# Fifteen instead of ten pairs of an FFN's up projection in seven half-size products, with weight sums made by adding transfers

## The chip, the cores and the metric

One core of a Trainium2 chip runs the whole program in one launch. The engines are TensorE (PE; its weight loads are PEld), VectorE (DVE), ScalarE (ACT), GpSimd (POOL) and SyncE (SP), which here only issues transfers. The metric is device time in microseconds, the median of several runs.

## The reference

A trunk of two layers over 512 tokens of width 1024, all in float32: a gated linear recurrence in layer 0, RWKV-7 time mixing in layer 1, each followed by the same channel mixer, then a final norm. The change touches the channel mixer alone:

```python
def _conv_ffn(x, norm, w_up, conv_w, conv_b, w_down):
    h = _rmsnorm(x, norm)
    u = jnp.einsum('btd,df->btf', h, w_up)                      # 1024 -> 2 x 3072
    gate = _causal_dwconv(u[..., :D_FF], conv_w, conv_b)        # 3 taps
    hid = jax.nn.gelu(gate, approximate=True) * u[..., D_FF:]
    return jnp.einsum('btf,fd->btd', hid, w_down)               # 3072 -> 1024

for layer in range(DEPTH):                                      # DEPTH = 2
    x = x + (_rglru_block if layer % 2 == 0 else _rwkv7_block)(x, ...)
    x = x + _conv_ffn(x, ...)
return _rmsnorm(x, final_norm)
```

## The kernel before

Every float32 matrix is split into a rounded part `hi` (ScalarE, a CAST) and the rest `lo` (VectorE, a subtraction), and a product is three matmuls, `mm3` (L54): hi with hi, hi with the operand's lo, lo with hi. Weights come from memory in pieces of 512 KB (`raw`), through one tag `b4` of 21 buffers that holds pieces, split pieces and the eight operand blocks `xs`. `plan_weights` writes down the order of all pieces; `weights_load` issues their loads on SP's queue in that order; a load starts when the buffer that it was given has been let go by its last reader. Pieces of the plan marked as a pair's own are split by that pair, all others by `weights_split` and taken by `next_weights`. The framework places each engine's instructions in one fixed order; an engine works through its own in that order and waits on semaphores.

`ffn(l, ...)` works on 12 *pairs*: pair n is 256 columns of the gate half of `w_up` and the same 256 of the other half. There are two kinds.

- `Whole`: four products of 24 matmuls of 512 tokens, G0, U0 (first 512 rows of `w_up` into the banks accG and accU), G1, U1 (the other 512 rows).
- `Halves`: the four blocks (two halves of the rows, gate and up) times two halves of the tokens, H = 256, written with seven products in place of eight (Winograd's form of Strassen's scheme). Each is 24 matmuls of 256 tokens. Products are named 1, 5, 6, 2, 7, then 4, 3, in the banks accA (1, 6, 7, 4), accF (5, 3) and accD (2). Products 1, 2 and 3 read `xs`; 5, 6, 7 and 4 read sums of operand blocks (`xt`) that `operands()` makes once for each FFN. Their weights are the pieces and sums of them: four tensor_tensor on VectorE per pair before (S1, S2, one in place, S4; L726 to L729). After a product, ScalarE copies accA (`s`), VectorE combines the banks, and `gate` convolves (four scalar_tensor_tensor, L678) and applies gelu.

`HALVES = (3, 5, 7, 9, 11)` in both FFNs. In a *period* run an even pair, an odd pair and `down(n, ...)`, the down projection of the two pairs before: two groups of 512 columns of `w_down`, each of two pieces (four products of six matmuls per piece, one bank each for four blocks). After the first piece of the first group, `between` runs the odd pair's products 4 and 3; at the end of that group `then` prepares the next pair's first weights. In the second FFN VectorE adds the down projection to `xtok` (L830). `products` sets the order of products, and `ahead` places the splits of the product after the next ahead of each.

Of the kernel before, what the change touches and what calls it, by code (L numbers as in the profile page):

```python
# [16 lines left out]
P = 128  # L17
# [14 lines left out]
HALVES = (3, 5, 7, 9, 11)  # L32
# [12 lines left out]
class Kernel:  # L45
# [54 lines left out]
    def plan_weights(self):  # L100
# [4 lines left out]
        def add(w, r0, c0, k=2, quad=False):  # L105
            plan.append((w[r0 : r0 + k * P, c0 : c0 + D // k].rearrange("(k p) c -> p k c", p=P), k, quad))
# [46 lines left out]
    def weights_load(self, upto):  # L153
        while self.n_load < min(upto, len(self.plan)):
            i = self.n_load
            src, k, _ = self.plan[i]
# [419 lines left out]
    def ffn(self, l, xs, finish, after=None):  # L576
        nc, tc = self.nc, self.tc
        last = l == 1
        with tc.tile_pool(name=f"ffn{l}", bufs=1) as pool:
# [43 lines left out]
            def operands():  # L623
# [6 lines left out]
                stt = nc.vector.scalar_tensor_tensor  # L630
                for k in range(4):
# [5 lines left out]
                    stt(f[:, 0], x2[:, H:], gain(4 + k), d[:, 1], ALU.mult, ALU.add)  # L637
                    parts(t2, k, f[:, 0])
                    stt(f[:, 1], x2[:, 0:H], gain(4 + k), f[:, 0], ALU.mult, ALU.subtract)
# [22 lines left out]
            tt = nc.vector.tensor_tensor  # L662
# [51 lines left out]
            class Halves(Pair):  # L714
# [3 lines left out]
                def weights(pair, p):  # L718
                    if p == 1:
                        i = quads[pair.n]  # L720
                        self.weights_load(i + 4)
                        pair.f = dict(zip((1, 7, 4, 2), [self.loaded.pop(i + j) for j in range(4)]))
                    f = pair.f
                    if p == 1:
                        f[5], f[6], f[3] = (self.b4(F32, (4, 256), name) for name in ("S1", "S2", "S4"))
                        tt(f[5], f[7], f[4], ALU.add)  # L726
                        tt(f[6], f[5], f[1], ALU.subtract)
                        tt(f[7], f[1], f[7], ALU.subtract)
                        tt(f[3], f[6], f[2], ALU.subtract)  # L729
# [3 lines left out]
                    pair.w[p] = hi, lo  # L733

                def product(pair, p):
# [19 lines left out]
                    if p == 7:  # L755
                        tt(s[7], s[7], bank["F"], ALU.subtract)
                        tt(gp[:, :, 2 + H :], s[7], rb(H, T), ALU.mult)
                    if p == 4:
                        tt(gp[:, :, 2 : 2 + H], bank["A"], rb(0, H), ALU.mult)
                        for e in range(2):  # L760
                            pair.gate(e)
                    if p == 3:
                        tt(s[6], s[6], bank["F"], ALU.subtract)
# [8 lines left out]
            quads = self.quads[l * 12 : l * 12 + 12]  # L772
            pairs, hids = {}, []
            kind = lambda n: Halves if n in HALVES else Whole
            seq = [(n, p) for n in range(12) for part in kind(n).order for p in part]
            made, at = [0], [0]
# [9 lines left out]
            def products(upto, more=2):  # L786

                while True:
# [4 lines left out]
                    if p == "G0" and n + 1 in HALVES:  # L793
                        self.weights_load(quads[n] + 8)
# [4 lines left out]
                    if p == 7:  # L799
                        self.weights_split(quads[n] + 6)  # L800
# [58 lines left out]

            for n in range(3, 12, 2):  # L860
# [4 lines left out]
                down(n, 2 * n - 6, 4 if n < 11 else 8, lambda: products((n, 3)), lambda: ahead(at[0] + 2))  # L865
# [889 lines left out]
```

## Time and profile before

| | |
|---|---|
| median of 3 runs | 1296.62 us (1294.75 to 1297.82) |
| the profiled execution | 1296.44 us, of which the instructions' span is 1294.7 |
| PE, DVE, ACT, POOL busy | 98%, 74%, 51%, 5% of the span |
| granted TensorE clock | 0.997 |
| read from memory | 114.44 MB, 92 GB/s with the writes |

PE, DVE, ACT and POOL are the four engines' busy times; a matmul's own duration is longer than the distance to the next one, because they are pipelined, so lengths of stretches are taken from the chain of waits, which holds what ended last at every moment. SPq and POOLq are the queues of transfers that SP and GpSimd issue; "to landing" is from issue until the data is there. In a row of a timeline stand start, length, engine, line, operation, output<-inputs.

### The profile page before, as it was taken

What the parts mean: (1) busy time and instruction counts of PE and PEld (TensorE: products, weight loads), DVE (VectorE), ACT (ScalarE), POOL (GpSimd) and SP (SyncE); (2) the same over time, 40 slices, a digit from 0 to 9 for tenths busy, and PEclk for the clock granted to TensorE, in tenths of its full rate; (3) what the DMA queues carried; (4) which work ended last, traced back from release to release, by engine and by line L of the source; (5) the groups of instructions that cost most, each with busy time, mean ns of one, the idle gap of its engine ahead of it and who ended that gap; (6) DMA issues with size and microseconds to landing.
All of it is one profiled execution on the core that took longest, in us unless ns stands there. A gap on an engine that the chain in (4) does not pass through costs nothing.

```text
span 1294.7 us, 22291 instructions
## 1 busy us (share of the span) xinstructions
PE 1266.9 (98%) x9259; PEld 1068.0 (82%) x9259; DVE 962.0 (74%) x1440; ACT 662.9 (51%) x1070; POOL 64.8 (5%) x112
## 2 busy tenths in 40 slices
PE   9999999999999999999899998899999999999997
PEld 8777888989888888877678887778889898988886
DVE  5998678767676777788999867777877666676754
ACT  6797455434344343568845468655644343443442
POOL 3000000000000000010002031210000000000000
PEclk9999999999999999999999999999999999999999
DMA  7322341515151513422212112132314151505131
GB/s 221 111 58 90 98 128 36 161 35 163 33 163 32 172 41 102 155 74 76 80 41 87 54 58 83 44 99 80 106 43 153 44 165 31 175 21 178 35 130 65
DMA packets 96710, 120.40 MB, mean 93 GB/s; under 512 B 9499, under 2 KB 70629, under 8 KB 96481
## 3 DMA queue, kind: packets, MB, share of 16 engines
q1 hardware_dynamic: 95248, 117.20, 28.6%
q8 instruction: 72, 1.18, 0.4%
q10 hardware_dynamic: 576, 1.05, 0.2%
q0 software_dynamic: 784, 0.74, 0.2%
q14 instruction: 30, 0.24, 0.1%
HBM read 114.44 MB, written 4.52 MB: 92 GB/s over the span
## 4 chain that ended last, share of the span: by engine, by line
PE 85%; DVE 9%; ACT 4%; issue 2%; POOL 0%; DMA 0%; POOLq 0%; ACTq 0%; DVEq 0%
PE acc L54 27%; PE accU L54 12%; PE accG L54 12%; PE accA L54 9%; PE accF L54 4%; PE acc L827 3%; PE acc L826 3%; PE acc L825 3%; PE accD L54 2%; DVE wl L97 1%; DVE X L1280 1%; DVE mt L947 1%; PE s L1394 1%; PE pd L1476 1%; DVE DA L1278 1%
## 5 line engine op out<-in xcount | busy, mean ns | idle before, releaser
L94 ACT CAST wh<-raw 128x1024 fp32r<-128x1024 f32 (+1 forms) x161 | 165.9, 1042 | 200.9 <-PE acc L54 55.6
L97 DVE TENSOR_TENSOR wl<-raw,wh 128x1024 fp32r<-128x1024 f32 (+1 forms) x161 | 195.5, 1220 | 95.3 <-ACT wh L94 81.7
L54 PE MATMUL accG<-xs,wh 128*128 128x512 f32 x448 | 138.8, 391 | 0.0
L54 PE MATMUL accU<-xs,wh 128*128 128x512 f32 x448 | 138.6, 391 | 0.0
L54 PE MATMUL acc<-hid,wh 128*128 128x512 f32 x384 | 119.7, 395 | 0.0
L54 PEld LDWEIGHTS accG<-xs,wh 128*128 128x128 f32 x448 | 83.7, 188 | 17.4
L54 PEld LDWEIGHTS accU<-xs,wh 128*128 128x128 f32 x448 | 83.7, 188 | 17.1
L54 PE MATMUL accG<-xs,wl 128*128 128x512 f32 x224 | 87.3, 390 | 0.0
L54 PE MATMUL accU<-xs,wl 128*128 128x512 f32 x224 | 87.3, 390 | 0.0
L54 PEld LDWEIGHTS acc<-hid,wh 128*128 128x128 f32 x384 | 71.2, 188 | 17.0 <-ACT wh L94 0.3
L54 PE MATMUL accA<-xt,hi 128*128 128x256 f32 x480 | 83.4, 277 | 0.0
L54 PE MATMUL acc<-xs,wh 128*128 128x512 f32 x256 | 81.1, 398 | 0.0
L732 DVE TENSOR_TENSOR lo<-raw,hi 128x1024 fp32r<-128x1024 f32 x40 | 48.3, 1220 | 40.2 <-PE accU L54 40.2
L678 DVE SCALAR_TENSOR_TENSOR cv<-gpad,pv,cv 128x512 f32<-128x512 f32 x96 | 69.0, 747 | 12.3 <-ACT cv L676 11.8
L827 PE MATMUL acc<-wl,hid 128*128 128x512 f32 (+1 forms) x200 | 77.2, 386 | 0.0
L826 PE MATMUL acc<-wh,hid 128*128 128x512 f32 (+1 forms) x200 | 77.0, 385 | 0.0
L825 PE MATMUL acc<-wh,hid 128*128 128x512 f32 (+1 forms) x200 | 76.7, 383 | 0.0
L54 PE MATMUL acc<-hid,wl 128*128 128x512 f32 x192 | 74.8, 395 | 0.0
L54 PEld LDWEIGHTS accA<-xt,hi 128*128 128x128 f32 x480 | 73.2, 188 | 0.9
L731 ACT CAST hi<-raw 128x1024 fp32r<-128x1024 f32 x40 | 42.1, 1051 | 57.7 <-PE accG L54 49.6
L54 PE MATMUL accA<-xt,lo 128*128 128x256 f32 x240 | 66.3, 276 | 0.0
L54 PE MATMUL acc<-mix,wh 128*128 128x512 f32 x192 | 59.6, 394 | 2.9 <-ACT wh L94 2.9
(413 smaller groups left out, 2970.7 us busy)
## 6 DMA issues: line engine op xcount, KB each, us to landing
raw<-in_ffn_w_up_dram SPq DMA_DIRECT2D x96, 512.0 KB, 3.9
raw<-in_ffn_w_down_dram SPq DMA_DIRECT2D x48, 512.0 KB, 4.0
raw<-in_rwkv_w_rkv_dram SPq DMA_DIRECT2D x24, 512.0 KB, 3.7
raw<-in_lru_w_in_dram SPq DMA_DIRECT2D x16, 512.0 KB, 4.1
raw<-in_lru_w_out_dram SPq DMA_DIRECT2D x8, 512.0 KB, 3.7
raw<-in_rwkv_w_out_dram SPq DMA_DIRECT2D x8, 512.0 KB, 3.5
xd<-x SPq DMA_DIRECT2D x8, 256.0 KB, 2.0
AR<-xd SPq DMA_DIRECT2D x1, 2048.0 KB, 9.0
```

Source lines behind the costliest of these rows:

```text
L54: mm = lambda *a, **kw: self.nc.tensor.matmul(ps, *a, skip_group_check=more, **kw)
L94: put = (self.nc.vector.tensor_copy if dve else self.nc.scalar.copy)(hi, src)
L97: self.nc.vector.tensor_tensor(lo, src, hi.bitcast(F32), ALU.subtract)
L678: nc.vector.scalar_tensor_tensor(cv, pair.gp[:, e, j : j + T], cw(j), cv, ALU.mult, ALU.add)
L731: nc.scalar.copy(hi, f[p])
L732: tt(lo, f[p], hi.bitcast(F32), ALU.subtract)
L825: nc.tensor.matmul(ps, hh[:, s], wh[:, k, m], start=kk == 0, stop=False)
L826: nc.tensor.matmul(ps, hl[:, s], wh[:, k, m], start=False, stop=False)
L827: nc.tensor.matmul(ps, hh[:, s], wl[:, k, m], start=False, stop=kk == blocks - 1)
L947: nc.vector.scalar_tensor_tensor(mt[:, 1:], h[:, cb, : T - 1], self.vec("rwkv_mix", i * 8 + cb), mt[:, 1:], ALU.mult, ALU.add)
L1278: nc.vector.tensor_tensor(w, A[:, s + 1 :, s : s + 1].to_broadcast([P, n, j]), X[:, s : s + 1, 0:j].to_broadcast([P, n, j]), ALU.mult)
L1280: nc.vector.tensor_tensor(X[:, s + 1 :, 0:j], X[:, s + 1 :, 0:j], w, ALU.add)
```

## The change

What it does, in five parts.

1. `HALVES` becomes a set for each FFN: (3, 5, 7, 9, 10, 11) for the first, (3, 4, ..., 11) for the second. Pair 10 of the first and pairs 4, 6, 8, 10 of the second change from `Whole` to `Halves`.
2. The signs of the seven products are turned, so that all sums of weights are additions: 5 is a sum of two pieces, 7 of two, 6 is 5 plus 1, 3 is 6 plus 2, and 4 is a piece. Operand sums and the combination after the products take the other sign (`minus`, a few subtractions turned to additions, two multiplications by `rb` to scalar_tensor_tensor with -1).
3. Three of the four sums leave VectorE. For 5 and 7 `weights_load` loads one piece on SP's queue and issues a second transfer on GpSimd's queue that adds the other piece in place; for 3 GpSimd adds a piece onto the weights of 6 once these are split. VectorE keeps one sum, 6 (L737).
4. So a pair by halves loads five pieces on SP's queue and three on GpSimd's, eight in place of four.
5. Where both pairs of a period go by halves, the odd pair's product 1 is placed ahead of the even pair's product 4, and loads are asked for at new points (`products`, `between`, `then`).

```diff
-HALVES = (3, 5, 7, 9, 11)
+HALVES = ((3, 5, 7, 9, 10, 11), (3, 4, 5, 6, 7, 8, 9, 10, 11))
...
                 for n in range(2 * six, 2 * six + 2):
                     self.quads.append(len(plan))
-                    i = int(n in HALVES)
-                    for half, r in ((i, 0), (1 - i, 0), (0, 512), (1, 512)):
-                        add(up, r, half * DFF + n * 256, 4, bool(i))
+                    a = lambda i, j: piece(up, j * 512, (1 - i) * DFF + n * 256, 4)
+                    if n in HALVES[l]:
+                        for first, more in (((0, 0), None), ((1, 1), (1, 0)), ((0, 1), None), ((1, 0), (0, 0)), ((1, 1), None)):
+                            plan.append((a(*first), 4, True, more and a(*more)))
...
+            if more is not None:
+                self.nc.gpsimd.dma_start(raw, more, accum_op=ALU.add)
...
                 def weights(pair, p):
+                    i = quads[pair.n]
                     if p == 1:
-                        i = quads[pair.n]
                         self.weights_load(i + 4)
-                        pair.f = dict(zip((1, 7, 4, 2), [self.loaded.pop(i + j) for j in range(4)]))
+                        pair.f = dict(zip((1, 5, 2, 7), [self.loaded.pop(i + j) for j in range(4)]))
                     f = pair.f
-                    if p == 1:
-                        f[5], f[6], f[3] = (self.b4(F32, (4, 256), name) for name in ("S1", "S2", "S4"))
-                        tt(f[5], f[7], f[4], ALU.add)
-                        tt(f[6], f[5], f[1], ALU.subtract)
-                        tt(f[7], f[1], f[7], ALU.subtract)
-                        tt(f[3], f[6], f[2], ALU.subtract)
+                    if p == 6:
+                        tt(f[1], f[5], f[1], ALU.add)
+                        f[6] = f[3] = f[1]
+                    if p == 7:
+                        self.weights_load(i + 5)
+                        f[4] = self.loaded.pop(i + 4)
                     hi, lo = self.b4(F32R, (4, 256), f"hi{p}"), self.b4(F32R, (4, 256), f"lo{p}")
                     nc.scalar.copy(hi, f[p])
                     tt(lo, f[p], hi.bitcast(F32), ALU.subtract)
                     pair.w[p] = hi, lo
+                    if p == 6:
+                        nc.gpsimd.dma_start(f[3], self.plan[i + 2][0], accum_op=ALU.add)
...
-                        tt(gp[:, :, 2 + H :], s[7], rb(H, T), ALU.mult)
+                        stt(gp[:, :, 2 + H :], s[7], -1.0, rb(H, T), ALU.mult, ALU.mult)
...
+            for n in range(4, 12, 2):
+                if n in HALVES[l] and n + 1 in HALVES[l]:
+                    seq.remove((n + 1, 1))
+                    seq.insert(seq.index((n, 4)), (n + 1, 1))
...
-                    if p == "G0" and n + 1 in HALVES:
-                        self.weights_load(quads[n] + 8)
+                    if n % 2 == 0 and n + 1 in HALVES[l] and p in ("G0", 5, 2, 7):
+                        self.weights_load(quads[n + 1] + {5: 1, 2: 2}.get(p, 4))
...
-                    if p == 7:
-                        self.weights_split(quads[n] + 6)
+                    if n % 2 and p in (2, 7):
+                        (self.weights_load if p == 2 else self.weights_split)(behind[n] + 2)
...
+            def between():
+                products((n, 3))
+                if n + 1 in HALVES[l]:
+                    self.weights_load(quads[n + 1] + 2)
+            def then():
+                if len(seq) > at[0]:
+                    self.weights_split(self.n_used + 2)
+                ahead(at[0] + 2)
...
-                down(n, 2 * n - 6, 4 if n < 11 else 8, lambda: products((n, 3)), lambda: ahead(at[0] + 2))
+                down(n, 2 * n - 6, 4 if n < 11 else 8, between, then)
```

Line numbers in the following rows of before are those of the profile; those of after are some 8 to 34 higher for the same statement (L678 is L690, L732 is L744, L97 stays, L830 is L853). Names are those of the code with a buffer number: `wl` and `wh` are split pieces of `w_down`, `lo1` the lo part of the weights of product 1, `cv` the gate's convolution, `raw` a piece.

VectorE in the second FFN, inside the down projection that follows pair 5, from the odd pair's last bank to the splits for the second column group. Before (`wl158` and `wl159` are the pieces of that group, `wl160` is the next whole pair's first piece):

```order
L757 TENSOR_TENSOR gpad1_9200<-s_10457,rb_9286 128x2x256
L97 TENSOR_TENSOR wl158_10574<-raw158_10477,wh158_10573 128x1024
L97 TENSOR_TENSOR wl159_10612<-raw159_10571,wh159_10611 128x1024
L759 TENSOR_TENSOR gpad1_9200<-accA_10313,rb_9286 128x2x256
L97 TENSOR_TENSOR wl160_10618<-raw160_10609,wh160_10617 128x1024
L678 SCALAR_TENSOR_TENSOR cv_10529<-gpad1_9200,pv_78,cv_10529 128x512
L678 SCALAR_TENSOR_TENSOR cv_10534<-gpad1_9200,pv_78,cv_10534 128x512
L678 SCALAR_TENSOR_TENSOR cv_10529<-gpad1_9200,pv_78,cv_10529 128x512
L678 SCALAR_TENSOR_TENSOR cv_10534<-gpad1_9200,pv_78,cv_10534 128x512
L763 TENSOR_TENSOR s_10397<-s_10397,accF_10344 128x512
```

And now, at the same place (`raw169` and `raw170` are the first two pieces of pair 6, the second one summed by a transfer; `wl167` is the first piece of the second column group):

```order
L772 SCALAR_TENSOR_TENSOR gpad1_9293<-s_10650,rb_9379 128x2x256
L744 TENSOR_TENSOR lo1_10705<-raw169_10694,hi1_10704 128x1024
L774 SCALAR_TENSOR_TENSOR gpad1_9293<-accA_10422,rb_9379 128x2x256
L737 TENSOR_TENSOR raw169_10694<-raw170_10696,raw169_10694 128x1024
L744 TENSOR_TENSOR lo5_10745<-raw170_10696,hi5_10744 128x1024
L690 SCALAR_TENSOR_TENSOR cv_10734<-gpad1_9293,pv_78,cv_10734 128x512
L690 SCALAR_TENSOR_TENSOR cv_10739<-gpad1_9293,pv_78,cv_10739 128x512
L690 SCALAR_TENSOR_TENSOR cv_10734<-gpad1_9293,pv_78,cv_10734 128x512
L690 SCALAR_TENSOR_TENSOR cv_10739<-gpad1_9293,pv_78,cv_10739 128x512
L778 TENSOR_TENSOR s_10586<-s_10586,accF_10531 128x512
L97 TENSOR_TENSOR wl167_10781<-raw167_10666,wh167_10780 128x1024
```

The split for the second group has moved from ahead of the gate's operations to behind them, and the next pair's sum, which reads an added piece, stands ahead of both.

VectorE further on, in the even pair 6 itself. Before, a whole pair with the four sums for pair 7 ahead of it:

```order
L726 TENSOR_TENSOR S1_10745<-raw165_10709,raw166_10711 128x1024
L727 TENSOR_TENSOR S2_10746<-S1_10745,raw164_10707 128x1024
L728 TENSOR_TENSOR raw165_10709<-raw164_10707,raw165_10709 128x1024
L729 TENSOR_TENSOR S4_10747<-S2_10746,raw167_10713 128x1024
L732 TENSOR_TENSOR lo1_10753<-raw164_10707,hi1_10752 128x1024
L97 TENSOR_TENSOR wl163_10757<-raw163_10705,wh163_10756 128x1024
L702 TENSOR_TENSOR gpad0_9199<-accG_10679,rb_9286 128x512
```

And now (`raw174` and `raw175` are pair 7's first two pieces, `raw173` is pair 6's last; `lo4` and `lo3` in these rows belong to pair 6, `lo1`, `lo5`, `lo6` to pair 7):

```order
L744 TENSOR_TENSOR lo1_10977<-raw174_10936,hi1_10976 128x1024
L737 TENSOR_TENSOR raw174_10936<-raw175_10968,raw174_10936 128x1024
L744 TENSOR_TENSOR lo4_11007<-raw173_10934,hi4_11006 128x1024
L767 TENSOR_TENSOR s_10903<-s_10903,accD_10980 128x512
L744 TENSOR_TENSOR lo3_11039<-raw169_10694,hi3_11038 128x1024
L744 TENSOR_TENSOR lo5_11070<-raw175_10968,hi5_11069 128x1024
L771 TENSOR_TENSOR s_11034<-s_11034,accF_10909 128x512
L744 TENSOR_TENSOR lo6_11111<-raw174_10936,hi6_11110 128x1024
```

Pair 7's sum stands ahead of pair 6's last two splits; the three other sums are gone from VectorE.

GpSimd's queue, from the norm of the second FFN on. Before:

```order
L1508 TENSOR_TENSOR bv_8910<-x_68,bon1_6070 128x512
L1511 TENSOR_TENSOR mu_8904<-var_8905,mhalf_76 128x8
L324 TENSOR_TENSOR rs_9247<-ms_9245,mhalf_76 128x4
L1698 DMA fg_12233<-in_final_norm_dram 128x1024
L1714 TENSOR_TENSOR fss_12235<-fss_12235,mhalf_76 128x1 x4
```

And now, as far as pair 6:

```order
L334 TENSOR_TENSOR rs_9340<-ms_9338,mhalf_76 128x4
L168 DMA raw147_9755<-in_ffn_w_up_dram 128x4x256
L168 DMA raw149_9760<-in_ffn_w_up_dram 128x4x256
L748 DMA raw146_9753<-in_ffn_w_up_dram 128x4x256
L168 DMA raw156_10077<-in_ffn_w_up_dram 128x4x256
L168 DMA raw158_10082<-in_ffn_w_up_dram 128x4x256
L748 DMA raw155_10075<-in_ffn_w_up_dram 128x4x256
L168 DMA raw161_10348<-in_ffn_w_up_dram 128x4x256
L168 DMA raw163_10353<-in_ffn_w_up_dram 128x4x256
L748 DMA raw160_10316<-in_ffn_w_up_dram 128x4x256
L168 DMA raw170_10696<-in_ffn_w_up_dram 128x4x256
L168 DMA raw172_10701<-in_ffn_w_up_dram 128x4x256
```

Where GpSimd had nothing between the norm and the end, it now issues three adding transfers a pair, in one queue: two for pieces as they are loaded (L168), one for the weights of product 3 (L748).

More of the change, by code (lines that the diff above doesn't have):

```diff
@@ L636, in operands @@
                     parts(n1, k, d[:, 1])
[L637 removed]
+                    stt(f[:, 0], x2[:, H:], minus[:, k : k + 1], d[:, 1], ALU.mult, ALU.subtract)
                     parts(t2, k, f[:, 0])
[L639 removed]
+                    stt(f[:, 1], x2[:, 0:H], minus[:, k : k + 1], f[:, 0], ALU.mult, ALU.subtract)
                     parts(t4, k, f[:, 1])
@@ L661, in ffn @@
             rb = lambda u, v: rbs[0][:, u:v].unsqueeze(1).to_broadcast([P, 2, v - u])
-            tt = nc.vector.tensor_tensor
+            tt, stt = nc.vector.tensor_tensor, nc.vector.scalar_tensor_tensor
             class Pair:
@@ L762, in product @@
                     if p == 3:
-                        tt(s[6], s[6], bank["F"], ALU.subtract)
+                        tt(s[6], s[6], bank["F"], ALU.add)
                         if not last:
```

24 lines of the change are left out of this document (17 added, 7 removed).

## The prediction

> **What bounds the kernel now.** I read the page's totals first, then the chain of waits over one stretch of the second FFN, then that stretch's busy times, then single rows of VectorE and of the transfers.
>
> ```profile
> span 1294.7 us, 22291 instructions
> PE 1266.9 (98%) x9259; PEld 1068.0 (82%) x9259; DVE 962.0 (74%) x1440; ACT 662.9 (51%) x1070; POOL 64.8 (5%) x112
> PEclk9999999999999999999999999999999999999999
> ```
>
> TensorE is busy for 98% of the span at full granted clock, so the only cheap gain is fewer matmul columns. The chain of waits of one period (pair 4 whole, pair 5 by halves, the down projection of pairs 2 and 3) holds TensorE alone; a row is its start, its length, the bank and the count of matmuls:
>
> ```profile
> 1011.23 5.46 PE accG L54 x24
> 1016.69 5.44 PE accU L54 x24
> 1022.13 5.44 PE accG L54 x24
> 1027.57 5.44 PE accU L54 x24
> 1033.01 2.87 PE accA L54 x24
> 1035.88 2.74 PE accF L54 x24
> 1038.62 2.72 PE accA L54 x24
> 1041.34 2.86 PE accD L54 x24
> 1044.20 2.75 PE accA L54 x24
> 1046.95 0.23 PE acc L825
> ...
> 1052.56 2.75 PE accA L54 x24
> 1055.31 2.86 PE accF L54 x24
> 1058.17 0.23 PE acc L825
> ...
> 1075.03 1.14 PE accG L54 x5
> ```
>
> Each row begins where the one before ends: nothing is waited for, so work taken from VectorE or ScalarE gains nothing here, and every wait that the change brings is paid in full. The busy times of the same stretch (PE, PEld, DVE, ACT, POOL, granted clock, DMA share, GB/s) show how much cover there is:
>
> ```profile
> 1011.06:1074.87 63.81, 63.81 (x362) 55.65 (x361) 42.96 (x50) 24.93 (x30) 0.00 (x0) 1.00 0.31 100
> ```
>
> **The gain.** A whole pair is 5.46 + 3 x 5.44 = 21.78 us, a pair by halves 2.87 + 2.74 + 2.72 + 2.86 + 2.75 + 2.75 + 2.86 = 19.55 us. Each converted pair saves 2.23 us, and five are converted (pair 10 of the first FFN; 4, 6, 8 and 10 of the second): 11.15 us. That is all of the gain.
>
> **What is covered.** The ten pairs that were by halves lose three of four weight sums each (some 3.5 us of VectorE); the chain has no VectorE there, so this is worth nothing. Of them five (3, 5, 7, 9 of the first FFN, 3 of the second) still follow a whole pair: their loads are asked for after its G0, some 16 us (U0, G1 and U1) before product 1, so their adding transfers are hidden by that pair's matmuls. Signs: the two scalar_tensor_tensor that replace multiplications are 0.06 us longer each, off the chain; `minus` is one small instruction. Loads: a pair by halves moves eight pieces where it moved four, so a period of two such pairs has 20 in place of 12; the share of 0.31 becomes 0.52, or 0.67 if an added piece costs double: transfers as such do not become the bound.
>
> **The cost: two places where VectorE waits for an adding transfer.** They exist only where both pairs of a period go by halves, which is five times. There a load can't start before the product that held its buffer ends, the addition waits for that load, and VectorE's sum for product 6 (L737) waits for the addition, with the next splits queued behind it. On SP's queue the pair's later pieces stand behind the held load, but their buffers come free later still. GpSimd has nothing else to do there (0.00 busy above), so its queue delays only its own next additions. The prices:
>
> ```profile
> raw<-in_ffn_w_up_dram SPq DMA_DIRECT2D x96, 512.0 KB, 3.9
> tgd<-lf SPq DMA_DIRECT2D x1, 64.0 KB, 1.6
> fg<-in_final_norm_dram POOLq DMA_DIRECT2D x1, 512.0 KB, 7.6
> DMA to landing us min/median/max: 3.6/5.2/6.8
> 1230.06:1237.66 7.60, 7.60 (x68) 7.60 (x68) 3.19 (x4) 2.69 (x3) 0.65 (x1) 1.00 0.73 254
> ```
>
> The fourth row is GpSimd's small parameter loads (L262), the last the stretch in which `fg` landed. No adding transfer is in this trace; call its time from issue to landing L. Low end: the quickest small one of GpSimd's queue, 3.6, plus what 512 KB add to a small one on SP's, 3.9 - 1.6 = 2.3: 5.9 us, if the target is not read separately. Reading the target too, one after the other, adds 2.3 again: 8.2. High end: `fg`, the nearest row (same size, same queue), plus 2.3: 9.9. But `fg` landed in a crowd (DMA share 0.73 against 0.31), so I go below it: **L = 7.0**, half way between one read and two without a crowd.
>
> VectorE and ScalarE, start to start where they run without idle time:
>
> ```profile
> 1014.14 1.23 DVE L727 TENSOR_TENSOR S<-S,raw 128x1024 f32<-128x1024 f32 x1
> 1015.29 1.22 DVE L728 TENSOR_TENSOR raw<-raw,raw 128x1024 f32<-128x1024 f32 x1
> 1032.24 0.74 DVE L678 SCALAR_TENSOR_TENSOR cv<-gpad,pv,cv 128x512 f32<-128x512 f32 x1
> 1032.90 1.22 DVE L732 TENSOR_TENSOR lo<-raw,hi 128x1024 fp32r<-128x1024 f32 x1
> 1034.04 0.69 DVE L97 TENSOR_TENSOR hid<-s,hid 128x512 fp32r<-128x512 f32 x1
> 1034.64 0.68 DVE L708 TENSOR_TENSOR s<-accU,ge 128x512 f32<-128x512 f32 x1
> 1036.84 0.57 ACT L750 COPY s<-accA 128x512 f32<-128x512 f32 x1
> 1054.71 1.05 ACT L94 CAST wh<-raw 128x1024 fp32r<-128x1024 f32 x1 [1.29 <-DVE wl L97]
> 1057.08 2.73 DVE L678 SCALAR_TENSOR_TENSOR cv<-gpad,pv,cv 128x512 f32<-128x512 f32 x4
> 1061.71 1.22 ACT L769 CAST hid<-s 128x512 fp32r<-128x512 f32 x2 [1.23 <-DVE s L768]
> ```
>
> So a split or sum of 1024 takes 1.15, a scalar_tensor_tensor of 512 takes 0.66 (2.65 for four), a tensor_tensor of 512 takes 0.60; 1.22 until a consumer may start. Zero is the start of product 1 of the even pair. By the chain's lengths product 1 ends at 2.87, the odd pair's last product 7 at 33.49, its product 3 at 44.71, and the down projection's second column group (four banks, L853) begins at 50.33; its third matmul, the first that needs `wl`, comes 0.46 later, at 50.8.
>
> *Place 1, down projection.* By the code and the built order, the next even pair's second piece is loaded when the odd pair's product 7 ends: 33.5 + 3.9 = 37.4, added by 37.4 + L. Then VectorE does the sum (1.15), lo5 (1.15), four gate operations (2.65), s (0.60) and the `wl` that is needed at 50.8 (1.22): 6.77. No stall while L is under 50.8 - 37.4 - 6.77 = 6.6. Before, that `wl` stood ahead of the gates and was split here, while the group began here:
>
> ```profile
> 1049.79 1.22 DVE L97 TENSOR_TENSOR wl<-raw,wh 128x1024 fp32r<-128x1024 f32 x1 [0.77 <-ACT wh L94]
> 1063.79 0.23 PE acc L825
> ```
>
> That was a cover of 13 us; with the landing of the addition at L = 0 it would still be only 0.3 us, because VectorE can't begin lo1 and the gate evacuation before product 4 ends at 41.85.
>
> *Place 2, inside the two pairs.* The odd pair's second piece is loaded when product 1 of the even pair ends: 2.9 + 3.9 = 6.8, added by 6.8 + L. Behind the sum VectorE has eight more splits, seven tensor_tensor, two scalar_tensor_tensor, four gate operations, and then the down projection's first `wl`: 9 x 1.15 + 7 x 0.60 + 2 x 0.66 + 2.65 + 1.22 = 19.7. It is needed at 33.49 + 0.46 = 33.95: no stall while L is under 7.4. Past it the wait doubles, because product 3's addition is issued after lo6 (6.95 behind the first landing) and lands L later, with 5.1 (hi3, two casts, a copy, `wh`, `wl`: 1.05 + 1.22 + 0.57 + 1.05 + 1.22) behind it: 13.75 + 2L + 5.1 = 33.95 at L = 7.55.
>
> In the first FFN extra multiplications by `rb` stand in both runs (two of 0.60 at place 1, three at place 2): no stall under 5.4 and 5.6.
>
> **The sum.** At L = 7.0: 4 x 0.4 at place 1 of the second FFN, none at its place 2, 1.6 + 1.4 in the first FFN: 4.6 us. 1296.44 - 11.15 + 4.6 = 1289.9; that execution lies 0.2 us under the median of 1296.62, so **1290.0 us**. At 5.9 the stalls are 0.8 and the time 1286.3; at 8.2 they are 4 x 1.6 + 4 x 1.3 + 2.8 + 2.6 = 17.0 and it is 1302.5; at 9.9 they are 4 x 3.3 + 4 x 4.7 + 4.5 + 4.3 = 40.8, and 1326.
>
> [...]
>
> **The rivals.** *All hidden:* L stays under 6; the time is 1285.5 to 1287. For it: the quiet stretches (share 0.31) and the low end of 5.9. Against: `fg`. *The additions come too late:* mechanism of places 1 and 2 with both reads in full; it decides from L = 7.8, where 4 x 1.2, 4 x 0.5 and 4.6 in the first FFN eat up the 11.15. With L = 8.2 to 9.9 the kernel takes 1302.5 to 1326. For it: `fg` at 7.6 without any addition; against: its crowd. [...] *Just balanced:* L of 7.6 to 8.0, 1294 to 1299, within 0.2% (2.6 us, about what a measurement of this kernel can tell from no change).
>
> **The chances.** All hidden 0.25, partly hidden as forecast (1287 to 1294) 0.36, balanced 0.13, too late 0.26. Faster 0.61, same 0.13, slower 0.26. The range goes from the all-hidden end with its play of a microsecond, 1284.5, to two full reads, 1303; the forecast case alone is 1287 to 1294.
>
> **What would show it.** The five pairs' chain rows at 2.7 to 2.9 us each with 24 matmuls, G and U rows gone from them; the adding transfers' row in the DMA issues gives L directly. At place 1 VectorE's idle time ahead of L737 should end on the DMA, and TensorE should wait for `wl` L97 at the start of the second column group, about 0.4 us each time; none in the pairs that follow a whole pair. I am wrong if ScalarE, held up by a CAST of an added piece, is what TensorE waits for, if GpSimd's issues queue up among themselves, or if waits appear ahead of whole pairs, where I put none.

## The result and the profile after

The changed kernel takes **1324.42 us** (median of 5 runs, 1323.28 to 1329.03) against 1297.69 us before (1294.75 to 1298.92): ratio 1.0221, 95% interval 1.0208 to 1.0233. It is 2.2% slower, where 1290.0 us and faster was forecast. The profiled execution took 1324.42 us at a span of 1322.7 us, 28.0 us more than before. One run further below, 2490.87 us of twenty_buffers, is far off the others of its kernel and left out of the medians.

The page of the changed kernel, its totals, clock, queues and the landing times of the two kinds of weight transfers (last column of the last two rows, median):

```profile
span 1322.7 us, 23253 instructions
PE 1268.9 (96%) x9619; PEld 1080.7 (82%) x9619; DVE 957.8 (72%) x1447; ACT 682.6 (52%) x1100; POOL 122.8 (9%) x157
PEclk9999999999999999999998999999999999899999
q1 hardware_dynamic: 103168, 125.06, 29.8%
q0 software_dynamic: 24544, 24.33, 12.1%
raw<-in_ffn_w_up_dram SPq DMA_DIRECT2D x111, 512.0 KB, 4.5
raw<-in_ffn_w_up_dram POOLq DMA_DIRECT2D x45, 512.0 KB, 5.9
```

L, the unknown of the prediction, is 5.9 us: its low end, at which it put the time at 1286.3. Yet TensorE, which hardly waited before, now waits. The groups of TensorE's instructions in the second FFN from pair 4 on say for what (busy, mean ns of one, idle time ahead of it and who ended it):

```profile
L54 PE MATMUL accA<-xt,hi 128*128 128x256 f32 x384 | 67.5, 278 | 2.9 <-ACT s L765 2.9
L848 PE MATMUL acc<-wh,hid 128*128 128x512 f32 x125 | 51.6, 413 | 3.6 <-ACT wh L94 3.6
L850 PE MATMUL acc<-wl,hid 128*128 128x512 f32 x125 | 49.9, 411 | 7.9 <-DVE wl L97 7.9
L54 PE MATMUL accF<-xs,hi 128*128 128x256 f32 x128 | 23.7, 285 | 2.5 <-DVE s L771 2.5
```

I added up, matmul by matmul, what the time from start to start exceeds the undisturbed pitch (0.23 us for 512 columns, 0.11 for 256: in the chain of before 24 of them take 5.44 and 2.74 us, though by its own record one of 512 lasts 0.39). Longer steps are stalls; steps of up to about twice the pitch are slow matmuls.

| | forecast | stalls | slow matmuls |
|---|---|---|---|
| place 1, second FFN (4 times) | 1.6 | 16.0 | 5.5 |
| place 2, second FFN (4 times) | 0 | 7.8 | 1.2 |
| both places, first FFN (once) | 3.0 | 8.2 | 0.7 |
| pairs that follow a whole pair | 0 | 0 | 0 |

Together 39.3 us, less the 11.15 us of the gain: 28.1, the measured 28.0. Outside the five periods with two pairs by halves no stretch changed by more than 0.6 us.

**Place 1, read in the rows.** Around the down projection after pair 7, GpSimd, VectorE, ScalarE and TensorE (start, length, instruction; in brackets the idle time ahead and what ended it). Product 7 ends at 1126.88:

```profile
1136.19 1.28 POOL L168 DMA_DIRECT2D raw<-in_ffn_w_up_dram  x1 [21.42 <-DMA raw<-in_ffn_w_up_dram]
```
```profile
1136.41 0.68 DVE L774 SCALAR_TENSOR_TENSOR gpad<-accA,rb 128x512 f32<-128x512 f32 x1
1142.06 1.23 DVE L737 TENSOR_TENSOR raw<-raw,raw 128x1024 f32<-128x1024 f32 x1 [4.97 <-DMA raw<-in_ffn_w_up_dram]
1143.20 1.22 DVE L744 TENSOR_TENSOR lo<-raw,hi 128x1024 fp32r<-128x1024 f32 x1
1144.34 2.73 DVE L690 SCALAR_TENSOR_TENSOR cv<-gpad,pv,cv 128x512 f32<-128x512 f32 x4
1146.99 0.68 DVE L778 TENSOR_TENSOR s<-s,accF 128x512 f32<-128x512 f32 x1
1147.59 1.22 DVE L97 TENSOR_TENSOR wl<-raw,wh 128x1024 fp32r<-128x1024 f32 x1
```
```profile
1142.04 1.05 ACT L743 CAST hi<-raw 128x1024 fp32r<-128x1024 f32 x1 [7.54 <-DMA raw<-in_ffn_w_up_dram]
1143.00 1.52 ACT L688 ACTIVATE cv<-gpad,pv 128x512 f32<-128x512 f32 x2
1144.42 1.03 ACT L94 CAST wh<-raw 128x1024 fp32r<-128x1024 f32 x1
```
```profile
1143.25 0.40 PE L850 MATMUL acc<-wl,hid 128*128 128x512 f32 x1
1145.50 0.50 PE L848 MATMUL acc<-wh,hid 128*128 128x512 f32 x1 [1.86 <-ACT wh L94]
1145.84 0.40 PE L849 MATMUL acc<-wh,hid 128*128 128x512 f32 x1
1148.86 0.80 PE L850 MATMUL acc<-wl,hid 128*128 128x512 f32 x1 [2.61 <-DVE wl L97]
1149.45 0.63 PE L848 MATMUL acc<-wh,hid 128*128 128x512 f32 x1
1149.88 0.63 PE L849 MATMUL acc<-wh,hid 128*128 128x512 f32 x1
```

The mechanism is the one forecast: L737 and the CAST wait for the addition, and `wh` and `wl`, which need no addition at all, stand behind them in their queues. But the addition is issued 9.31 us after product 7's end, where 3.9 was taken. At place 2 it is 7.36 us (product 1 of pair 6 ends at 1092.97, the addition is issued at 1100.33). These are the longest of their kind: in the four periods of the second FFN it is 6.0, 8.8, 9.3 and 8.2 us at place 1, and 5.5, 7.4, 5.5 and 6.0 at place 2. From the product's end to the addition's landing it takes 12.7 to 15.1 us at place 1 and 11.3 to 13.2 at place 2; the forecast had 3.9 + 7.0 = 10.9.

**Slow matmuls, and full transfer engines.** The last rows above have matmuls at 0.43 us from start to start (1149.45 to 1149.88) where 0.23 is usual. Two such stretches, and two with crowded transfers (stretch, its length, busy times of PE, PEld, DVE, ACT and POOL, granted clock, DMA share, GB/s):

```profile
1077.50:1081.00 3.50, 3.30 (x8) 2.63 (x9) 3.50 (x7) 2.19 (x4) 0.00 (x0) 0.55 0.00 0
1147.00:1151.00 4.00, 2.14 (x5) 1.76 (x6) 4.00 (x7) 3.20 (x6) 0.00 (x0) 0.50 0.00 0
1094.00:1100.00 6.00, 6.00 (x55) 6.00 (x54) 1.56 (x2) 2.42 (x3) 0.00 (x0) 1.00 1.09 347
1128.00:1138.00 10.00, 10.00 (x69) 9.19 (x68) 3.19 (x5) 1.05 (x1) 1.28 (x1) 1.00 0.80 256
```

In three of the four periods a stall at place 1 has a step of 3.02 us from start to start (from 1074.68, 1145.84 and 1214.66), and 0.1 us after its end (twice) or within it the granted clock fell to 0.50 (at 1077.84, 1146.11 and 1217.79, for 3.41, 6.83 and 3.41 us): the slow matmuls cost 1.7 to 1.8 us on top of each. In the fourth period, with steps of 2.03 and 1.64 us, the clock stayed at 1.00. And where the loads in question are under way, the transfer engines are full (1.09; packets are counted by their start, so a short stretch can pass 1) or nearly so (0.80), while the mean share is 0.62 to 0.64 in three such periods and 0.54 in the last.

### The profile page after: what moved, and what is told of

Same layout as the page of the kernel before. It is cut to its first block, busy times and chain, and to the rows that moved or that the text cites. A ratio compares the mean times of both kernels' runs of the same rounds, so it can differ in the third digit from the quotient of the medians.

```text
span 1322.7 us, 23253 instructions
## 1 busy us (share of the span) xinstructions
PE 1268.9 (96%) x9619; PEld 1080.7 (82%) x9619; DVE 957.8 (72%) x1447; ACT 682.6 (52%) x1100; POOL 122.8 (9%) x157
## 3 DMA queue, kind: packets, MB, share of 16 engines
q0 software_dynamic: 24544, 24.33, 12.1%
## 5 line engine op out<-in xcount | busy, mean ns | idle before, releaser
L743 ACT CAST hi<-raw 128x1024 fp32r<-128x1024 f32 x105 | 109.8, 1050 | 194.3 <-DMA raw<-in_ffn_w_up_dram 75.9
L97 DVE TENSOR_TENSOR wl<-raw,wh 128x1024 fp32r<-128x1024 f32 (+1 forms) x141 | 170.9, 1219 | 50.9 <-ACT wh L94 39.7
L744 DVE TENSOR_TENSOR lo<-raw,hi 128x1024 fp32r<-128x1024 f32 x105 | 127.7, 1221 | 97.9 <-PE accA L54 57.8
L54 PE MATMUL accA<-xt,hi 128*128 128x256 f32 x720 | 126.1, 278 | 5.2 <-ACT s L765 5.2
L54 PEld LDWEIGHTS accA<-xt,hi 128*128 128x128 f32 x720 | 109.4, 188 | 7.5 <-ACT s L765 6.6
L54 PE MATMUL accA<-xt,lo 128*128 128x256 f32 x360 | 99.8, 277 | 0.9 <-DVE lo L744 0.9
L54 PE MATMUL accG<-xs,wh 128*128 128x512 f32 x288 | 89.4, 392 | 0.0
L54 PE MATMUL accU<-xs,wh 128*128 128x512 f32 x288 | 89.4, 391 | 0.0
L168 POOL DMA_DIRECT2D raw<-in_ffn_w_up_dram x30 | 38.6, 1285 | 415.5 <-DMA raw<-in_ffn_w_up_dram 191.5
L690 DVE SCALAR_TENSOR_TENSOR cv<-gpad,pv,cv 128x512 f32<-128x512 f32 x96 | 68.2, 747 | 10.2 <-ACT cv L688 9.9
L54 PEld LDWEIGHTS accA<-xt,lo 128*128 128x128 f32 x360 | 67.6, 188 | 1.5 <-DVE lo L744 1.5
L54 PEld LDWEIGHTS accG<-xs,wh 128*128 128x128 f32 x288 | 53.6, 188 | 11.0
L54 PEld LDWEIGHTS accU<-xs,wh 128*128 128x128 f32 x288 | 53.6, 188 | 10.9
```

The costliest lines, as they stand in the source:

```text
L54: mm = lambda *a, **kw: self.nc.tensor.matmul(ps, *a, skip_group_check=more, **kw)
L97: self.nc.vector.tensor_tensor(lo, src, hi.bitcast(F32), ALU.subtract)
L168: self.nc.gpsimd.dma_start(raw, more, accum_op=ALU.add)
L690: nc.vector.scalar_tensor_tensor(cv, pair.gp[:, e, j : j + T], cw(j), cv, ALU.mult, ALU.add)
L743: nc.scalar.copy(hi, f[p])
L744: tt(lo, f[p], hi.bitcast(F32), ALU.subtract)
```

## The experiments

| run | us | ratio to before (95%) |
|---|---|---|
| ten_pairs | 1295.45 | 0.9988 (0.9979 to 0.9998) |
| no_additions | 1285.48 | 0.9917 (0.9904 to 0.9931) |
| no_addition_for_3 | 1321.23 | 1.0196 (1.0182 to 1.0210) |
| held_behind | 1297.40 | 1.0006 (0.9997 to 1.0015) |
| held_further | 1291.17 | 0.9963 (0.9950 to 0.9975) |
| sums_on_vector | 1303.07 | 1.0053 (1.0040 to 1.0066) |
| sums_on_vector_held | 1300.01 | 1.0028 (1.0017 to 1.0039) |
| added_piece_first | 1316.84 | 1.0165 (1.0143 to 1.0187) |
| copies_for_additions | 1305.70 | single run |
| added_first_held | 1294.10 | 0.9989 (0.9977 to 1.0001) |
| own_buffer | 1302.62 | 1.0045 (1.0032 to 1.0059) |
| twenty_buffers | 1351.74 | 1.0417 (1.0399 to 1.0434) |
| own_buffer_held | 1303.54 | 1.0062 (1.0041 to 1.0083) |
| eighteen_pairs_held | 1284.07 | 0.9907 (0.9890 to 0.9923) |
| eighteen_added_first_held | 1290.10 | 0.9953 (0.9940 to 0.9966) |

**Is it the extra pairs, and is it the additions?**

Ten_pairs changes the first line; no_additions takes out the two others.

```diff
-HALVES = ((3, 5, 7, 9, 10, 11), (3, 4, 5, 6, 7, 8, 9, 10, 11))
+HALVES = ((3, 5, 7, 9, 11), (3, 5, 7, 9, 11))
```
```diff
-                self.nc.gpsimd.dma_start(raw, more, accum_op=ALU.add)
...
-                        nc.gpsimd.dma_start(f[3], self.plan[i + 2][0], accum_op=ALU.add)
```

> The changed kernel with only the ten pairs of before by halves (3, 5, 7, 9, 11 in both FFNs); signs, adding transfers and load points as changed. In it every pair by halves follows a whole pair. My theory (the loss lies only where two pairs by halves follow each other): no wait for an adding transfer, 1295 to 1298 us, within 0.2% of before. Rival (adding transfers on GpSimd's queue cost wherever they stand, by traffic or by the order on VectorE): 30 additions at a us or so each, 1305 us or more.

> Fifteen pairs as changed, but all adding transfers left out (the products 5, 7 and 3 then work on unsummed weights; plain loads, splits and products all stay). My theory (what TensorE waits for is VectorE and ScalarE held up by an addition that lands late): the 39 us of waiting and slow matmuls go, 1285 to 1288 us. Rival (the new order of products and the more crowded plain loads are to blame): most of the loss stays, 1312 us or more.

Both came as expected. Thirty adding transfers behind whole pairs cost nothing (1295.45). Without any addition the fifteen pairs take 1285.48 us: the gain of 11.15 is there in full (1296.6 - 11.15 = 1285.5). So the 39 us need both, an addition and two pairs by halves in a row.

**Is it the order in which work is queued behind the addition?** In held_behind L737 (`total`), and the CAST and split for product 5 (`parts`), are tied behind instructions of the same engine that need no addition: for an even pair the last splits of the down projection's weights (`self.last`), for an odd pair the even pair's CAST and split for product 3 (`.last`). A tie sets the order of issue and waits for nothing. The ties are made where a pair by halves comes before. Besides, `ahead` stops one product earlier at product 3 of an odd pair; what that does by itself was not tried. The ties:

```diff
...
+                    if pair.n - 1 in HALVES[l] and p in (5, 6):
+                        last = pairs[pair.n - 1].last if pair.n % 2 else self.last
+                        for ins, prev in zip(parts if p == 5 else (total,), last if p == 5 else last[1:]):
+                            behind_of(self.tc, ins, prev)
...
```

Held_further ties the odd pair's CAST also behind the COPY of its own product 1, and the split and L737 behind the even pair's sum for product 7.

> Nothing left out. At both places the CAST and the split for product 5 and the sum for product 6 (L737) are put, on ScalarE and VectorE, behind the work that does not need the addition: behind the two splits of the down projection's second column group (even pair), behind the split for product 3 of the even pair (odd pair). My theory (the additions themselves come early enough for their own products, 28 and 22 us after the loads are asked for; only work queued behind them was late): 1285 to 1292 us. Rival (the transfers of two pairs by halves are too much for the engines in that time): the wait moves to products 5 and 6 themselves, 1310 us or more.

> As held_behind, and inside a period (odd pair) the CAST for product 5 stands also behind ScalarE's COPY of its own product 1 and so behind the even pair's COPY of product 7, and L737 behind the even pair's sum for product 7. In held_behind TensorE still waited there once a period, 1.6 to 3.2 us, for that COPY, which stood behind the CAST that waits for the addition. My theory (all 39 us are work queued behind a late addition): no wait is left, 1284 to 1288 us. Rival (some weights of the pair itself are late): 1291 us or more.

Held_behind regained 27 of the 39 us: place 1 lost every stall, though its additions landed as late as before (13.1 to 14.7 us after the product). At place 2 TensorE still waited, 1.5 to 3.4 us a period. ScalarE's rows there show for what, the COPY out of the bank that TensorE writes next, behind the CAST that waits for the addition:

```profile
1090.66 1.04 ACT L746 CAST hi<-raw 128x1024 fp32r<-128x1024 f32 x1 [5.43 <-DMA raw<-in_ffn_w_up_dram]
1091.61 0.58 ACT L773 COPY s<-accA 128x512 f32<-128x512 f32 x1
```
```profile
PE accA L58 <- ACT s L773: 2.5, 1, 2.5
```

The last row is TensorE's wait for that COPY (us in total, times, longest).

Held_further, with the COPY ahead, took 1291.17 us, 33 of the 39 regained and 0.4% faster than before, though not the 1284 to 1288 expected; the number lies in the rival's range (1291 or more), but the rival's mechanism does not show: no product's own weights were late. What is left in the second FFN is `wl`, behind the 18 us of VectorE work that begin with the late sum:

```profile
L862 PE MATMUL acc<-wl,hid 128*128 128x512 f32 x129 | 50.9, 398 | 2.5 <-DVE wl L101 2.5
```

**Are the additions late because the loads ahead of them are?** Three runs move the landing. In added_piece_first the piece that gets an addition is first in its pair's loads; in copies_for_additions `accum_op` is dropped, at L748 too; in no_addition_for_3 only L748 is left out.

```diff
-for first, more in (((0, 0), None), ((1, 1), (1, 0)), ((0, 1), None), ((1, 0), (0, 0)), ((1, 1), None)):
+for first, more in (((1, 1), (1, 0)), ((0, 0), None), ((0, 1), None), ((1, 0), (0, 0)), ((1, 1), None)):
-self.nc.gpsimd.dma_start(raw, more, accum_op=ALU.add)
+self.nc.gpsimd.dma_start(raw, more)
```

> Only the third adding transfer of a pair (L748, for product 3) left out. It runs from 1089 to 1096 us in the period of pairs 6 and 7, right ahead of the plain load of the odd pair's second piece (issued 1093.2, landed 1099.6 us). My theory (that load lands late since the 16 engines are busy with what was asked for before it): the load lands some 3 us earlier at place 2, so most of the 14 us lost at place 2 goes, the 26 us lost at place 1 stay: 1309 to 1315 us. Rival (the load is late for a reason of its own, its queue or its latency): place 2 as before, 1321 to 1326 us.

> Only the order of the first two loads of a pair by halves is exchanged: the piece that gets an addition is asked for first, product 1's piece second. Additions, sums and splits as changed. In the changed kernel the first of the two lands 2.3 us ahead of the second at both places (1133.4 and 1135.6; 1097.3 and 1099.6 us). My theory (the mis-sized term is the time from the end of a product to the landing of the plain load, 7.4 and 9.3 us where 3.9 were taken, by the queue of loads ahead of it): additions 2.3 us earlier, stalls at place 1 from about 4 us and 1.4 us of slow matmuls to 2 us each, at place 2 to none, 1294 to 1300 us. Rival (the loss hangs on the length of the addition itself, or on the order on VectorE alone): 1318 us or more.

> The adding transfers write over their target in place of adding to it (no accumulation; sizes, queue and times of issue as changed). Theory one (an addition keeps the engines busy twice as long as a load, 102 against 47 ns per 1 KB packet, and that is part of its 5.9 us): they land after some 4.2 us, and the time falls to 1303 to 1312 us. Theory two (the 5.9 us are GpSimd's issue and its queue, whatever the transfer does): 5.9 us as before, 1320 us or more.

The first came out as its rival said, 1321.23 us. In the period shown, with L748's transfer out of the way, the load at place 2 landed 4.79 us after its issue (1093.01), not 6.45 (1093.16), 1.7 us sooner, and in the first FFN 1.8 us sooner. In the three other periods L748's transfer has landed within 0.3 us of the load's issue, and leaving it out changed nothing there (4.8 to 5.3 us in both kernels). Place 2's stalls in the second FFN fell from 7.8 to 6.3 us, those at place 1 rose from 16.0 to 18.3. So that transfer explains part of two periods and no more. The second moved the additions by 0 to 1 us in place of 2.3 and the time by 7.6, to between the two ranges: issued earlier, the addition itself fell among the loads (7.1 us to landing, after 5.8). It told the two explanations apart poorly. The copies landed in 4.3 us and the time fell into the range of theory one:

```profile
q0 software_dynamic: 7264, 24.33, 5.9%
raw<-in_ffn_w_up_dram POOLq DMA_DIRECT2D x45, 512.0 KB, 4.3
```

What was open after that: lateness of the load, or the addition's own length and the order. Own_buffer makes the load earlier, and with it the addition, which stays as long:

```diff
-N4 = 21
+N4 = 20
...
+self.owned = [quads[n] + 1 for n in range(4, 12)] if last else ()
+self.own = lambda i: self.xsp.tile([P, 4, 256], F32, tag="own", name=f"raw{i}", bufs=1)
...
+                    if last and n % 2 and n < 11 and p == 6:
+                        self.piece_load(quads[n + 1] + 1)
...
+                if last and n < 11:
+                    self.piece_load(quads[n + 2] + 1)
```

The last two cuttings stand in `products` and in `then`; `piece_load` loads one piece out of the plan's order, and its addition with it.

> In the second FFN the piece of pairs 4 to 11 that gets product 5's addition has a buffer of its own (one, taken from the shared ones, 20 in place of 21) and is asked for earlier: the even pair's after product 6 of the odd pair before, the odd pair's in the down projection before its period. Additions, sums, splits and VectorE's order at the two places as changed. My theory (the mis-sized term is the time at which the plain load ahead of the addition lands): no late addition in the second FFN, so its 24 us of stalls and 7 us of slow matmuls go and the first FFN's 9 stay: 1292 to 1299 us. Rival (the order on VectorE and ScalarE costs even with early additions, or the additions' own 5.9 us do): 1315 us or more.

> The changed kernel with 20 shared buffers in place of 21, and nothing else: what the buffer given up in own_buffer costs by itself. My theory: loads wait for buffers longer, so additions come later still: 1325 to 1345 us. Rival (buffers do not set when the loads are asked for): 1323 to 1326 us.

In own_buffer the additions land 3 to 5 us ahead of the end of the product that they used to follow (pair 4's far earlier). On VectorE L737 still stands ahead of the gates and of `wl` (only lo5 moved, behind the gates), the additions still take 6.0 us, and in the second FFN, against its control with as many buffers, the waits are nearly gone. First own_buffer, then twenty_buffers, TensorE's groups from pair 4 on:

```profile
L54 PE MATMUL accA<-xt,hi 128*128 128x256 f32 x384 | 67.0, 277 | 0.0
L857 PE MATMUL acc<-wl,hid 128*128 128x512 f32 x144 | 55.4, 398 | 2.3 <-DVE wl L97 2.3
```
```profile
L54 PE MATMUL accA<-xt,hi 128*128 128x256 f32 x384 | 69.2, 282 | 5.3 <-ACT s L765 5.3
L54 PE MATMUL accA<-xt,lo 128*128 128x256 f32 x192 | 54.4, 283 | 11.0 <-DVE lo L744 11.0
L848 PE MATMUL acc<-wh,hid 128*128 128x512 f32 x125 | 53.8, 431 | 14.3 <-ACT wh L94 14.3
```

The difference of the two medians is 49.1 us; twenty_buffers itself lost more than the 1325 to 1345 us expected. Own_buffer's own median misses the range expected by 3.6 us, because of what the lost buffer costs elsewhere: the first FFN's stalls and slow matmuls there grew from 8.8 to 11.4 us, and the time between the two FFNs' up projections from 395.0 to 398.9.

Put together, second FFN, four periods (delay: from the product's end to the addition's landing; stalls without slow matmuls):

| run | delay, place 1 | stall | delay, place 2 | stall |
|---|---|---|---|---|
| twenty_buffers | 13.5 to 17.7 | 2.8 to 7.2 | 15.2 to 15.6 | 3.4 to 6.8 |
| changed | 12.7 to 15.1 | 3.2 to 5.2 | 11.3 to 13.2 | 1.3 to 2.9 |
| added_piece_first | 12.6 to 14.1 | 3.0 to 3.9 | 11.1 to 12.5 | 1.1 to 2.3 |
| copies_for_additions | 11.4 to 13.6 | 1.8 to 3.2 | 10.5 to 10.9 | 0.5 to 1.0 |
| own_buffer | -27 to -3 | 0 to 1.8 | -5.5 to -4.8 | 0 |

In the changed kernel, added_piece_first, copies_for_additions and no_addition_for_3, delay less stall is 9.5 to 10.8 us at place 1 and 9.7 to 10.2 at place 2, period by period: past about 10 us each microsecond of delay is one of stall. In twenty_buffers, with longer delays, it is 10.5 to 10.9 at place 1, but 8.5 to 12.0 at place 2, so there the rule is rough. (Of the 3.0 us of stalls left at place 1 in own_buffer most are the first group's first `wl`, 0.5 to 0.7 us each. The longest, 1.2 us after pair 7, is `wl` of the second group, and the chain of waits leads from it back to the plain load of product 1's piece, 7.25 us to landing:

```profile
1129.36 2.00 ACT L746 CAST hi<-raw 128x1024 fp32r<-128x1024 f32 x2 [8.56 <-DMA raw<-in_ffn_w_up_dram]
```

VectorE's gates and that `wl` stand behind this CAST's result.)

**Would VectorE be the better adder?** Sums_on_vector loads four pieces a pair and makes all four sums with tensor_tensor.

> The fifteen pairs with no adding transfers: four plain loads and four sums on VectorE a pair (the sum for product 5 into a buffer of its own), nothing held behind. Same result. My theory (the loss is the time from the end of the load to the end of the addition, with VectorE and ScalarE queued behind; VectorE is busy for 43 of 63 us of such a period, so 3 sums a pair more fit): 1285 to 1291 us, the rest of a wait where a plain load lands late. Rival (VectorE's work is short in such a period, which is why sums were moved to the transfers): 1297 us or more.

> sums_on_vector with the order of held_further. My theory: 1284 to 1288 us, the same as held_further within 0.2%. Rival (with four sums a pair the order leaves VectorE late for TensorE): 1292 us or more.

21 us better than the changed kernel, and still behind before: both lie in the ranges of their rivals, by which VectorE's time is short, and the order of held_further helps by 3 us only. TensorE's groups in sums_on_vector from pair 4 on:

```profile
L54 PE MATMUL accA<-xt,hi 128*128 128x256 f32 x384 | 67.9, 278 | 2.7 <-ACT s L765 2.7
L848 PE MATMUL acc<-wh,hid 128*128 128x512 f32 x116 | 46.1, 398 | 2.8 <-ACT wh L94 2.8
L850 PE MATMUL acc<-wl,hid 128*128 128x512 f32 x119 | 43.0, 398 | 1.4 <-DVE wl L97 1.4
```

VectorE, at 78% of the span, has the time on average; what delays its splits there I did not follow. With the same order the additions on GpSimd's queue are the better place for the sums, 1291.2 against 1300.0 us.

**Combinations.**

> added_piece_first and held_further together, fifteen pairs. In held_further VectorE still worked without a pause from the late addition at place 2 to the first split of the down projection, which TensorE waited for (0.8 to 1.7 us a period). My theory: with the addition 2.3 us earlier that goes too, 1285 to 1288 us, as without any addition (1285.5). Rival (something else than the additions is left): 1290 us or more.

> own_buffer with the order of held_further. My theory: the first FFN's stalls go too: 1285 to 1288 us. Rival (held_further's last 5 us come from something else than late additions, such as the split for the second column group late on VectorE): 1289 us or more.

> held_further with pairs 4, 6 and 8 of the first FFN by halves too: eighteen pairs. My theory: three times 2.23 us less than held_further, 1277 to 1282 us. Rival (the first FFN, with its extra multiplications by rb and other work in the down projections, has not the room): 1286 us or more.

> added_first_held with eighteen pairs (4, 6 and 8 of the first FFN too): 6.7 us below that, 1278 to 1281 us, which is below both kernels. Rival (the first FFN has no room for it): 1284 us or more.

Added_first_held missed, in its rival's range: with product 1's piece second, the CAST of that piece waits for its plain load (7.4 us in one period), and TensorE again for a COPY behind it (2.8 us in the second FFN). Own_buffer_held missed too, also in its rival's range: the single buffer is freed by the CAST and split that are held, so the next load waits for them, and its waits for the COPY are 3.9 us. Eighteen_pairs_held is the best of all, **0.9907 (0.9890 to 0.9923) of before**: three more pairs in the first FFN gave 7.1 us under held_further (forecast 6.7), and TensorE's share is back at 98%:

```profile
span 1281.0 us, 23745 instructions
PE 1251.3 (98%) x9835; PEld 1079.6 (84%) x9835; DVE 974.1 (76%) x1468; ACT 697.6 (54%) x1118; POOL 134.3 (10%) x166
```

Its median of 1284.07 lies a little above the 1277 to 1282 expected. Eighteen_added_first_held, in its rival's range too, is 6.0 us slower than eighteen_pairs_held, where added_first_held is 2.9 us slower than held_further; I did not follow the rest.

## Why the prediction was wrong, point by point

- **The gain, 5 x 2.23 = 11.15 us: right.** No_additions shows it undiminished.
- **Ten pairs behind whole pairs cost nothing: right** (ten_pairs; no stall there in the changed kernel either).
- **Places 1 and 2 as the only places, L737 waiting with splits queued behind it: right**, shown by held_behind and held_further with every addition left in.
- **L: 7.0 taken, 5.9 measured.** The error has the wrong sign for the result. That a second read adds 2.3 us was an estimate; no run shows an addition's reads one by one.
- **The load ahead of the addition, 3.9 us from the product's end: the step that failed.** From the product's end to the addition's issue it is 6.0 to 9.3 us at place 1 and 5.5 to 7.4 at place 2. The load itself takes 5.4 to 7.1 and 4.8 to 6.5 us to land; at place 1 it also stands on SP's queue behind the first piece's load, so that 1.7 us pass before its issue in three of four periods; and from its landing to the addition's issue go 0.56 to 0.71 us, to which the prediction gave nothing. With the measured delays the prediction's own arithmetic gives (12.7 + 14.6 + 15.1 + 14.0) - 4 x 10.5 = 14.4 us at place 1 of the second FFN, where 16.0 were measured, and (13.3 - 9.3) + (13.3 - 9.5) = 7.8 us in the first FFN, where it was 8.2.
- **Why these loads land late.** The 3.9 was a median over a kernel in which loads mostly came singly or in twos (74 of the 84 pieces of `w_up` whose landing shows were asked for with at most one other on its way). In the period shown five loads and L748's addition are asked for within 8 us at place 2 (1088.0 to 1095.8), five loads within 6 us at place 1 (1126.4 to 1132.3), and in such a crowd loads land 1.4 to 2.3 us apart. "Transfers as such do not become the bound" was argued from a mean share; the mean was as forecast (0.54 to 0.64; 0.52 to 0.67 was given), but in the microseconds that count the share was 1.09 at place 2 and 0.80 at place 1. That the crowd makes the loads late is read from these rows; by a run it is shown only for L748's transfer, in two periods: in the period shown 6.45 us to landing beside it and 4.79 without it.
- **The threshold at place 2, 11.3 us after the product: 1.3 us too lax.** Delay less stall is 10.0. TensorE waits there for ScalarE's COPY and VectorE's sums for product 7 (the groups by L765 and L771 above), not for `wl`. The prediction named this case, ScalarE held up by a CAST of an added piece, among what would make it wrong, but priced VectorE's queue alone; at place 1 too TensorE waited 3.6 us for ScalarE's `wh`. Here the threshold weighs more than the load: with the measured delays only pairs 7 and 11 pass 11.3 us clearly, by 1.9 and 0.8.
- **Slow matmuls after a stall: no term at all**, 7.4 us measured.

Of the 34.4 us between 1290.0 and 1324.4, place 1 of the second FFN has 14.4, place 2 there 7.8, the first FFN 5.2 and slow matmuls 7.4 (34.8 in all). The rival "the additions come too late" had the sign, the places and by chance the size (1326 at L = 9.9); it had the delay in the wrong transfer.

## What to carry to other kernels

Price a wait from the event that frees the buffer to the last landing, with every transfer asked for in those microseconds in line, not with the median landing time of a quieter kernel (3.9 us, where 4.8 to 7.1 were measured); the mean share of the transfer engines, 0.54 to 0.64, did not show the burst of 1.09. Before a piece of work that may wait for a transfer is put on an in-order engine, list what stands behind it: here tying three instructions a pair behind others (and one product's preparation a step later) was worth 33 us with every transfer left in. A load whose data is needed through two hops (load, then addition) may be asked for earlier, but see what that delays: in a buffer of its own it won 49.1 us over its control and still ended behind before, asked for first it won 7.6, and together with the better order it lost 2.9.

## What the runs showed of the hardware

- In the changed kernel an addition of 512 KB into SBUF in rows of 1 KB landed 5.9 us after its issue (median of 45), in copies_for_additions a copy of the same bytes on the same queue 4.3; GpSimd's issue took 1.28 us and 0.75; the queue's share of the engines was 12.1% and 5.9% for the same 24.33 MB, in 24544 and in 7264 packets. So the additions had smaller packets and took more of the engines' time. Of that time packet size explains little: in these traces an adding packet of 1 KB took 102 ns (median), a plain one of 1 KB on SP's queue 46, a plain one of 4 KB in copies_for_additions 159, 40 a KB. What makes the landing longer stays open.
- The additions took about twice the copies' share of the transfer engines, 12.1% (changed) against 5.9% (copies_for_additions), with the reservation on packets above.
- In the FFNs the granted clock fell to 0.50 with most steps of some 3 us from start to start (2.96 in added_piece_first, 3.09 and 3.23 in held_behind; in the changed kernel 0.1 us after two steps of 3.02 and 0.3 us into the third), not with 2.35 (changed) or 2.79 (held_behind). But twenty_buffers has it with 2.92 and not with 3.01 and 3.52, and no_addition_for_3 not with 3.68, so length alone does not decide. There the half clock lasted 3.41 us or twice that. In the traces of before and of the changed kernel all its beginnings lie whole multiples of 3.413 us apart (before: 637.94, 709.62 and 1293.30; changed: 644.35, 716.03, 1077.84, 1146.11, 1217.79 and 1320.19). What decides whether a stall brings it, no run shows.
- One buffer of 21 fewer cost 27.3 us (twenty_buffers against the changed kernel). The two profiled executions are 28.1 us apart: 19.2 us in the second FFN, 7.0 between the two FFNs' up projections, 1.6 in the first FFN.
